# Seven half-size block products for each pair of up-projection chunks, with the weight sums made by accumulating DMAs and the residual rows kept in DRAM

## The chip, the cores and the metric

The kernel runs on one core of a Trainium2 chip. The metric is the device time of one execution in microseconds (us), the median of several runs. All arithmetic is float32; a product that needs float32 accuracy is made of three matmuls of a faster 32-bit type.

## The reference

One layer of a hybrid diffusion model is computed for 640 tokens (128 of a prompt, 512 of a latent grid of width 64). Three mixers on one input projection are merged by gates and projected, a first normalisation follows, and then a gated convolutional feed-forward with a second one. The change lies in the last part:

```python
def _conv_ffn(h, w_up, w_dw, b_dw, w_down, latent):
    a, g = jnp.split(h @ w_up, 2, axis=-1)
    ...   # conv: 3x3 depthwise over the grid (or width 3 on the prompt), of a
    conv = conv + b_dw
    return (jax.nn.gelu(conv) * g) @ w_down

# in _layer
x = _layer_norm(alpha * x + g1 * mix, p['ln1_g'], p['ln1_b'])
h2 = (_norm32(x) * (1.0 + sc2) + sh2)
f = _conv_ffn(h2, p['w_up'], p['w_dw'], p['b_dw'], p['w_down'], latent)
x = _layer_norm(alpha * x + g2 * f, p['ln2_g'], p['ln2_b'])
```

D_MODEL is 1024 and D_FF 2816, so w_up is 1024 x 5632: 22 chunks of 128 columns for a and 22 for g. Chunk j of a and chunk j of g are called pair j here.

## The kernel before

**Split products.** A float32 matrix is held as a high part (a rounded cast, hi) and a low part (the rest, lo). `split` (L219) makes both for a loaded weight chunk of 128 x 1024: ACT casts it into `wh`, and `low` (L195) subtracts on DVE into `wl`. The load is a 512 KB DMA from `wst`, issued on SP into `raw`. `mm3` (L277 to 279) then issues three matmuls: hi by hi, hi by lo, lo by hi. A chunk of the up-projection takes 8 blocks of the inner dimension by 2 halves of 320 tokens by 3, which is 48 matmuls; a pair takes 96.

**The start of the feed-forward.** While the first normalisation is finished, a manual order (all three of PE, DVE and ACT, in `tc.manual_schedule`) transposes and modulates its result into `h2` (eight blocks of 128 x 640, hi and lo; `channel`, `last_channels`), channel by channel. Beside this, the chunks of pairs 0 to 2 are multiplied early: `open_up` loads and splits them, `first_up` issues their matmuls for 384 tokens and later for the other 256, and `land` copies the results from PSUM. `ada_rows` (L443) makes the rows of `g2` from column sums: ACT casts, DVE subtracts, PE sums over partitions by two matmuls with `ones`, and ACT copies from PSUM (L452). The residual `acc` (five tiles of 128 x 1024) lies in SBUF for the whole feed-forward.

**The parts.** The 22 pairs stand in PARTS of 6, 8 and 8. For each part, `expand(j)` calls `raise_` (two chunks by `proj_cm`, each copied from PSUM by ACT in L1511), `taps` (the convolution as one tensor_scalar, L1522, and eleven scalar_tensor_tensor, L1524 and L1534, on DVE) and `weigh` (gelu on ACT, L1540; the product with g on DVE, L1541; cast and low part of the result `h`, L1543 and L195). After the pairs of a part, `contract` multiplies by w_down for ten groups (five token tiles, two halves of 512 columns): 18 or 24 matmuls of 512 columns into PSUM, then two DVE operations (L1557, L1559) that scale by `g2` and add to `acc`. In the last part the second normalisation and the stores follow each token tile.

**The order around it.** Each engine runs its own instructions in order; waits on semaphores join them. Outside the manual blocks a scheduler has interleaved pairs: while PE multiplies pair j, DVE convolves pair j - 1 and splits weights for pair j + 1. `raw` has two buffers, and every third load goes to a third, `raw2`; `wh` and `wl` have four each.

An earlier stage of the kernel already makes products by seven half-size products (its tiles are `pair` and `kept`); its operations on 128 x 320 tiles (L1051, L1055) and its sums of activations (L230) are in the trace.

## Time and profile before

| | |
|---|---|
| time before, median of 3 runs | 1201.14 us (1199.91 to 1201.42) |
| the profiled execution, its own time | 1200.44 us |
| span of the profiled execution | 1198.4 us |
| PE busy | 1179.3 us, 98% of the span |
| DVE busy | 839.8 us, 70% |
| ACT busy | 448.4 us, 37% |
| POOL busy | 0.2 us, no DMA |
| mean granted clock of PE | 0.996 of full speed |
| up-projection matmuls (`up`) | 3 lines, 672 each |

A duration in the trace is that of one instruction from start to end. Instructions of one engine overlap a little, so a row of them takes less than the sum of durations. Where a timeline says `[0.79 <-ACT h L1543]`, the engine stood for 0.79 us until the cast of line 1543 had come. "Hole" in the prediction is a stretch in which PE stands.

### The profile page before, as it was taken

What the parts mean: (1) busy time and instruction counts of PE and PEld (TensorE: products, weight loads), DVE (VectorE), ACT (ScalarE), POOL (GpSimd) and SP (SyncE); (2) the same over time, 40 slices, a digit from 0 to 9 for tenths busy, and PEclk for the clock granted to TensorE, in tenths of its full rate; (3) what the DMA queues carried; (4) which work ended last, traced back from release to release, by engine and by line L of the source; (5) the groups of instructions that cost most, each with busy time, mean ns of one, the idle gap of its engine ahead of it and who ended that gap; (6) DMA issues with size and microseconds to landing.
All of it is one profiled execution on the core that took longest, in us unless ns stands there. A gap on an engine that the chain in (4) does not pass through costs nothing.

```text
span 1198.4 us, 18882 instructions
## 1 busy us (share of the span) xinstructions
PE 1179.3 (98%) x7751; PEld 1120.4 (93%) x7751; DVE 839.8 (70%) x1566; ACT 448.4 (37%) x724; POOL 0.2 (0%) x4
## 2 busy tenths in 40 slices
PE   8999999999999999999999999999999999999996
PEld 7899999999999999989999888898999988999986
DVE  7698666647677658579874678787377764667876
ACT  5566637424344322223333356442133321333320
POOL 0000000000000000000000000000000000000000
PEclk9999999999999999999999999999999999999999
DMA  9431212122125226245442423222222212322221
GB/s 350 181 106 54 71 54 71 54 71 66 49 95 196 90 75 207 89 158 177 145 137 71 158 71 120 75 71 77 82 72 78 81 36 71 124 71 71 72 71 53
DMA packets 35958, 120.35 MB, mean 100 GB/s; under 512 B 4120, under 2 KB 6552, under 8 KB 35872
## 3 DMA queue, kind: packets, MB, share of 16 engines
q1 hardware_dynamic: 35872, 119.16, 29.4%
q8 instruction: 60, 0.98, 0.3%
q14 instruction: 26, 0.21, 0.1%
HBM read 115.47 MB, written 3.67 MB: 99 GB/s over the span
## 4 chain that ended last, share of the span: by engine, by line
PE 88%; DVE 6%; ACT 3%; DMA 2%; issue 1%; SPq 0%; DVEq 0%; ACTq 0%
PE up L278 8%; PE up L277 8%; PE up L279 8%; PE gm L277 5%; PE gm L278 5%; PE gm L279 5%; PE dn L278 4%; PE dn L277 4%; PE dn L279 4%; PE pp L277 2%; PE pp L278 2%; PE pp L279 2%; PE pair L279 1%; PE pair L278 1%; PE rp L279 1%; PE rp L278 1%
## 5 line engine op out<-in xcount | busy, mean ns | idle before, releaser
L219 ACT CAST wh<-raw 128x1024 fp32r<-128x1024 f32 (+1 forms) x137 | 141.8, 1036 | 398.5 <-PE up L278 91.8
L195 DVE TENSOR_TENSOR wl<-raw,wh 128x1024 fp32r<-128x1024 f32 (+1 forms) x141 | 170.2, 1208 | 135.4 <-ACT wh L219 133.9
L278 PE MATMUL up<-go,wh 128*128 128x320 f32 (+2 forms) x672 | 208.7, 311 | 1.1 <-DVE go L195 1.1
L279 PE MATMUL up<-go,wl 128*128 128x320 f32 (+2 forms) x672 | 208.4, 310 | 0.5 <-DVE s11hv L307 0.5
L277 PE MATMUL up<-go,wh 128*128 128x320 f32 (+2 forms) x672 | 208.7, 311 | 0.0
L278 PEld LDWEIGHTS up<-go,wh 128*128 128x128 f32 x672 | 127.0, 189 | 2.2 <-DVE go L195 1.9
L279 PEld LDWEIGHTS up<-go,wl 128*128 128x128 f32 x672 | 126.9, 189 | 0.8 <-DVE wl L195 0.8
L277 PEld LDWEIGHTS up<-go,wh 128*128 128x128 f32 x672 | 127.0, 189 | 0.2
L277 PE MATMUL gm<-h,wh 128*128 128x320 f32 x384 | 121.4, 316 | 0.0
L278 PE MATMUL gm<-h,wh 128*128 128x320 f32 x384 | 119.0, 310 | 0.0
L279 PE MATMUL gm<-h,wl 128*128 128x320 f32 x384 | 118.7, 309 | 0.0
L1534 DVE SCALAR_TENSOR_TENSOR m<-m,par,m 128x441 f32<-128x441 f32 (+2 forms) x152 | 105.6, 695 | 4.1
L421 DVE SCALAR_TENSOR_TENSOR adac<-rawa,csil,adac 128x512 f32<-128x512 f32 x120 | 84.9, 746 | 10.0 <-DMA rawa<-in_wada 7.8
L277 PEld LDWEIGHTS gm<-h,wh 128*128 128x128 f32 x384 | 72.1, 188 | 1.7 <-issue 1.2
L278 PEld LDWEIGHTS gm<-h,wh 128*128 128x128 f32 x384 | 72.2, 188 | 0.3
L279 PEld LDWEIGHTS gm<-h,wl 128*128 128x128 f32 x384 | 72.1, 188 | 0.0
L278 PE MATMUL dn<-wl,h 128*128 128x512 f32 (+1 forms) x188 | 71.4, 381 | 0.0
L279 PE MATMUL dn<-wh,h 128*128 128x512 f32 (+1 forms) x188 | 70.8, 380 | 0.0
L277 PE MATMUL dn<-wh,h 128*128 128x512 f32 (+1 forms) x188 | 70.4, 380 | 0.0
L1557 DVE TENSOR_TENSOR ftmp<-dn,g 128x512 f32<-128x512 f32 (+1 forms) x32 | 20.8, 656 | 45.2 <-PE dn L279 45.2
L278 PEld LDWEIGHTS dn<-wl,h 128*128 128x128 f32 x188 | 35.4, 188 | 7.0 <-DVE wl L195 0.4
L277 PE MATMUL rp<-h,wh 128*128 128x320 f32 x128 | 41.7, 326 | 0.0
(420 smaller groups left out, 2701.3 us busy)
## 6 DMA issues: line engine op xcount, KB each, us to landing
raw<-in_wst SPq DMA_DIRECT2D x152, 512.0 KB, 3.5
rawa<-in_wada SPq DMA_DIRECT2D x32, 512.0 KB, 3.4
wa<-in_wada SPq DMA_DIRECT2D x16, 512.0 KB, 7.6
xa<-in_x SPq DMA_DIRECT2D x5, 512.0 KB, 3.5
xr<-in_x SPq DMA_DIRECT2D x5, 512.0 KB
out_y<-acc SPq DMA_DIRECT2D x10, 256.0 KB, 2.0
ttr<-in_ttab SPq DMA_DIRECT2D x2, 516.0 KB, 6.8
S<-in_state SPq DMA_DIRECT2D x8, 128.0 KB, 3.4
```

What stands on the lines that cost most here:

```text
L195: V.tensor_tensor(out, src, hi.bitcast(F32), op=ALU.subtract)
L219: A.copy(wh[:, 0:n], r)
L277: PE.matmul(out, lhsT=l[0], rhs=r[0], start=start, stop=False, skip_group_check=onto)
L278: PE.matmul(out, lhsT=l[0], rhs=r[1], start=False, stop=False, skip_group_check=onto)
L279: PE.matmul(out, lhsT=l[1], rhs=r[0], start=False, stop=stop, skip_group_check=onto)
L421: MAC.scalar_tensor_tensor(acc_[:, cd], r[:, i], s_, acc_[:, cd], op0=ALU.mult, op1=ALU.add)
L1534: V.scalar_tensor_tensor(cg[:, r0:r1, c0:c1], ag[:, r0 + r - 1:r1 + r - 1, c0 + c - 1:c1 + c - 1], tap(r, c), cg[:, r0:r1, c0:c1], op0=ALU ...
L1557: V.tensor_tensor(ftmp[:, 0:cn], p1[:, 0:cn], g2[:, cd, c], op=ALU.mult)
```

## The change

For pairs 3 to 21 the two chunks of a pair are taken as one product of a 256-column weight matrix with 640 tokens, and the blocks of it (two halves of the inner dimension, a and g, the near 320 and the far 320 tokens) are multiplied in a scheme of seven products of 12 matmuls, in place of eight. The scheme needs sums of weight halves, sums of halves of `h2`, and sums of results.

The weight sums are made by DMAs on POOL: in `up_weights` two 512 KB chunks are loaded on SP into `ra` and `rb`, and five DMAs of 256 KB (four of them accumulating, one a plain load over a used half) turn them into further sets; `r22` is a third load of 256 KB. Four splits give `wa`, `wc`, `wd` (128 x 1024 each) and `wb` (128 x 512). The sums of activations are made once, in `sum_halves` and `low_halves`, in the manual order behind `last_channels`; two more rows of casts and low parts, for the far half of `h2` and for the sums `s4`, stand behind the last `land`. The results are summed in PSUM where the scheme allows it, and otherwise on DVE (L1593, L1600, L1602).

`acc` is stored to DRAM (`x1d`) after the first normalisation, and its SBUF serves the sums and then the buffers `sraw` (5 of 128 x 1024) and `fm` (6 of 128 x 640). `contract` adds to `x1d` by accumulating DMAs on POOL; in the last part the rows are loaded back. `ada_rows` for `g2` becomes `ada_direct`, one float32 matmul in place of cast, low part and two matmuls. The first of the taps moves from DVE to ACT (L1614).

```diff
+FM, SRAW, FT = 6, 5, 2
...
+    def ada_direct(acc_, out, nh):
+        for cd in range(2):
+            pb = p1t("adab")
+            PE.matmul(pb, lhsT=ones.bitcast(F32), rhs=acc_[:, cd], start=True, stop=True)
...
-    accp = ctx.enter_context(tc.tile_pool(name="acc", bufs=1, reuse_waits="tile"))
+    kept_d = ctx.enter_context(tc.tile_pool(name="kd", bufs=1, space=bass.MemoryType.DRAM))
+    x1d = [kept_d.tile([P, D], F32, name=f"x1d{t}") for t in range(NT)]
+    accx = ExitStack()
+    accp = accx.enter_context(tc.tile_pool(name="acc", bufs=1, reuse_waits="tile"))
...
+                    nc.gpsimd.dma_start(out=x1d[t], in_=a)
...
+            s23 = [[mp.tile([P, T], F32R, tag="m", name=nm("s23")) for _ in range(2)] for _ in range(4)]
+            s4_ = [acc[k][:, 640:960] for k in range(4)]
+            s1_ = [acc[4][:, k * 320:(k + 1) * 320] for k in range(3)] + [acc[1][:, 320:640]]
+            def sum_halves(k):
+                x1, x2, s = acc[0][:, 0:T], acc[1][:, 0:T], acc[2 + k % 2][:, 0:T]
+                for x_, a in ((x1, h2[k]), (x2, h2[k + 4])):
+                    V.tensor_tensor(x_, a[0].bitcast(F32), a[1].bitcast(F32), op=ALU.add)
+                s2, s3 = s[:, 0:320], s[:, 320:]
+                V.tensor_tensor(s1_[k], x2[:, 320:], x1[:, 320:], op=ALU.subtract)
+                V.scalar_tensor_tensor(s2, s1_[k], -1.0, x1[:, 0:320], op0=ALU.mult, op1=ALU.subtract)
+                V.tensor_tensor(s3, x1[:, 0:320], x1[:, 320:], op=ALU.subtract)
+                V.scalar_tensor_tensor(s4_[k], s2, -1.0, x2[:, 0:320], op0=ALU.mult, op1=ALU.subtract)
+                A.copy(s23[k][0], s)
+            def low_halves(k):
+                low(s23[k][1], acc[2 + k % 2][:, 0:T], s23[k][0])
+            for k in range(4):
+                sum_halves(k)
+                if k:
+                    low_halves(k - 1)
+            low_halves(3)
...
-            ada_rows(late, g2_sums[0], g2, 0)
+            ada_direct(g2_sums[0], g2, 0)
...
+                hi, lo = sl(h2[k], slice(320, T))
+                A.copy(hi, s1_[k])
+                low(lo, s1_[k], hi)
+            t4 = [late.tile([P, 1024], F32R, tag="adak", bufs=2, name=nm("s4")) for _ in range(2)]
+            u4 = [late.tile([P, 512], F32R, tag=e, bufs=1, name=nm("s4")) for e in ("adah", "adal")]
+            s4 = []
+            for k in range(4):
+                hi, lo = [t[:, k * 320:(k + 1) * 320] for t in t4] if k < 3 else [t[:, 0:320] for t in u4]
+                A.copy(hi, s4_[k])
+                low(lo, s4_[k], hi)
+                s4.append((hi, lo))
+    accx.close()
...
+        def fm():
+            return pu.tile([P, T], F32, tag="fm", bufs=FM, name=nm("fm"))
+        def onto(o, i):
+            nc.gpsimd.dma_start(out=o, in_=i, accum_op=ALU.add)
+        def up_weights(j):
+            ia, ib = (plan.setdefault(("cm", "w_up", i * DFF + j * P), len(plan)) for i in range(2))
+            ra, rb = (pu.tile([P, 1024], F32, tag="sraw", bufs=SRAW, name=nm("sraw")) for _ in range(2))
+            f, s = slice(0, 512), slice(512, 1024)
+            nc.sync.dma_start(out=ra, in_=wst[ia])
+            nc.sync.dma_start(out=rb, in_=wst[ib])
+            wa = split(ra)
+            onto(rb[:, f], wst[ia][:, f])
+            nc.gpsimd.dma_start(out=ra[:, f], in_=wst[ib][:, f])
+            onto(rb[:, s], rb[:, f])
+            onto(ra[:, f], wst[ib][:, s])
+            wc = split(rb)
+            onto(ra[:, s], rb[:, s])
+            r22 = strm.tile([P, 1024], F32, tag="raw", name=nm("raw"))
+            nc.sync.dma_start(out=r22[:, f], in_=wst[ib][:, s])
+            wd = split(ra)
+            wb = split(r22[:, f], 512)
+            return wa, wb, wc, wd
+        near, far = slice(0, 320), slice(320, T)
+        a11, a12 = [[sl(h2[k + i], near) for k in range(4)] for i in (0, 4)]
+        s1, a22 = [[sl(h2[k + i], far) for k in range(4)] for i in (0, 4)]
+        s2, s3 = [sl(s, near) for s in s23], [sl(s, far) for s in s23]
...
-                else:
-                    a = mt()
-                    w = chunk("cm", "w_up", i * DFF + j * P)
-                    pp = ppt("up")
-                    proj_cm(pp, w, h2)
-                    A.copy(tv(a), pv(pp))
-                at.append(a)
-            return at
+                    at.append(a)
+            if at:
+                return at
+            wa, wb, wc, wd = up_weights(j)
+            a, g = fm(), fm()
+            pp = ppt("up")
+            xx, yy, vv = pp[:, 0, 0:320], pp[:, 1, 0:320], p1t("up")[:, 0:320]
+            def product(o, w, c0, acts, new):
+                for k in range(4):
+                    mm3(o, sl(w, slice(c0 + k * P, c0 + (k + 1) * P)), acts[k], bool(new) and k == 0, k == 3, not new)
+            product(xx, wa, 0, a11, 1)
+            A.copy(a[:, near], xx)
+            product(yy, wa, 512, a12, 1)
+            V.tensor_tensor(a[:, near], a[:, near], yy, op=ALU.add)
+            product(xx, wc, 512, s2, 0)
+            A.copy(g[:, near], xx)
+            product(vv, wc, 0, s1, 1)
+            A.copy(a[:, far], vv)
+            product(xx, wd, 0, s3, 0)
+            A.copy(g[:, far], xx)
+            V.scalar_tensor_tensor(g[:, far], g[:, far], -1.0, a[:, far], op0=ALU.mult, op1=ALU.subtract)
+            product(vv, wb, 0, s4, 0)
+            V.scalar_tensor_tensor(g[:, near], g[:, near], -1.0, vv, op0=ALU.mult, op1=ALU.subtract)
+            product(xx, wd, 512, a22, 0)
+            A.copy(a[:, far], xx)
+            return [a, g]
...
-            V.tensor_scalar(cv, a, tap(1, 1), pcol(PB_BDW, j), op0=ALU.mult, op1=ALU.add)
+            A.activation(cv, a, AF.Identity, bias=pcol(PB_BDW, j), scale=tap(1, 1))
...
+            if not last:
+                V.scalar_tensor_tensor(ftmp[:, 0:cn], p1[:, 0:cn], 1.0 / ALPHA, g2[:, cd, c],
+                                       op0=ALU.mult, op1=ALU.mult)
+                onto(x1d[t][:, c], ftmp[:, 0:cn])
+                return
...
+        acc = [pu.tile([P, D], F32, tag="sraw", bufs=SRAW, name=nm("acc")) for _ in range(NT)]
+        for t in range(NT):
+            nc.sync.dma_start(out=acc[t], in_=x1d[t])
+        ln = [[mt()[:, 0:512] for _ in range(2)] for _ in range(2)]
+        for i in range(2):
+            for nh in range(2):
+                nc.sync.dma_start(out=ln[i][nh],
+                                  in_=rows[2 + i:3 + i, nh * 512:(nh + 1) * 512].partition_broadcast(P))
```

First place: ACT, in the manual order behind the activations of the last channel. `adah` and `adab` belong to the rows of g2, `land` is the copy of a raised product, `s_...` are the sums of activations. Before:

```order
L467 ACTIVATE go_7716<-xT_1295_7996,mod 128x256
L447 CAST adah_8057<-adac_6660 128x512
L219 CAST wh_8265<-raw_8263 128x1024
L219 CAST wh_8322<-raw_8320 128x1024
L452 COPY g_7132<-adab_8061 128x512
L447 CAST adah_8065<-adac_6660 128x512
L452 COPY g_7132<-adab_8069 128x512
L1387 COPY land_8073<-up_7564 128x256
L1387 COPY land_8073<-up_7564 128x384
L1387 COPY land_8076<-up_7705 128x256
```

Now:

```order
L474 ACTIVATE go_7726<-xT_1295_8008,mod 128x256
L1498 CAST s_1298_8021<-acc_7129 128x640
L1498 CAST s_1300_8023<-acc_7130 128x640
L1498 CAST s_1302_8025<-acc_7129 128x640
L1498 CAST s_1304_8027<-acc_7130 128x640
L459 COPY g_7139<-adab_8109 128x512
L459 COPY g_7139<-adab_8112 128x512
L1398 COPY land_8115<-up_7574 128x256
L1398 COPY land_8115<-up_7574 128x384
L1398 COPY land_8118<-up_7715 128x256
```

Two weight casts, of chunks of pair 3, and the casts for g2 have gone, and the four casts of the sums stand ahead of the first copies of `adab` and `land`.

Second place: DVE, from the last channel's low parts to the weights of pair 3. Before, where `land` rows are taps of pairs 0 to 2:

```order
L195 TENSOR_TENSOR go_7717<-htmp_8005,go_7716 128x256
L195 TENSOR_TENSOR adal_8058<-adac_6660,adah_8057 128x512
L195 TENSOR_TENSOR wl_8266<-raw_8263,wh_8265 128x1024
L195 TENSOR_TENSOR wl_8323<-raw_8320,wh_8322 128x1024
L195 TENSOR_TENSOR adal_8066<-adac_6660,adah_8065 128x512
L1522 TENSOR_SCALAR m_8208<-land_8073,par 128x640
L1524 SCALAR_TENSOR_TENSOR m_8208<-land_8073,par,m_8208 128x127
L1534 SCALAR_TENSOR_TENSOR m_8208<-land_8073,par,m_8208 128x7x63
L195 TENSOR_TENSOR adal_8130<-adac_6872,adah_8129 128x512
L1524 SCALAR_TENSOR_TENSOR m_8208<-land_8073,par,m_8208 128x127
L1534 SCALAR_TENSOR_TENSOR m_8208<-land_8073,par,m_8208 128x448
L195 TENSOR_TENSOR wl_8398<-raw_8395,wh_8397 128x1024
```

Now, the end of the sums and, further on, the last taps ahead of the first low part of a weight of pair 3 (`sraw`):

```order
L196 TENSOR_TENSOR s_1317_8240<-acc_7127,s_1316_8239 128x320
L196 TENSOR_TENSOR s_1317_8240<-acc_7128,s_1316_8239 128x320
L196 TENSOR_TENSOR s_1317_8240<-acc_7129,s_1316_8239 128x320
L196 TENSOR_TENSOR s_1319_8242<-acc_7130,s_1318_8241 128x320
L1616 SCALAR_TENSOR_TENSOR fm_8257<-land_8115,par,fm_8257 128x127
L1626 SCALAR_TENSOR_TENSOR fm_8257<-land_8115,par,fm_8257 128x7x63
```

```order
L1616 SCALAR_TENSOR_TENSOR fm_8293<-land_7932,par,fm_8293 128x127
L1626 SCALAR_TENSOR_TENSOR fm_8275<-land_7775,par,fm_8275 128x448
L196 TENSOR_TENSOR h_8272<-fm_8257,h_8271 128x640
L1626 SCALAR_TENSOR_TENSOR fm_8275<-land_7775,par,fm_8275 128x7x63
L1626 SCALAR_TENSOR_TENSOR fm_8293<-land_7932,par,fm_8293 128x7x63
L196 TENSOR_TENSOR wl_8316<-sraw_8311,wh_8315 128x1024
```

Taps used to begin while the raised products ran, and weight low parts of pair 3 stood among them; now all taps stand behind the last sum, and 25 rows of pairs 0 to 2 (from L1616 on `fm_8257` to L1626 on `fm_8293`) lie between that sum's low part and the first weight low part of pair 3.

Third place: ACT in the up stage, one pair of part 1 (`sraw_9698` and `sraw_9699` are ra and rb of the next pair, `raw` its r22). Before:

```order
L219 CAST wh_9316<-raw_9314 128x1024
L1511 COPY m_9049<-up_9056 128x640
L1540 ACTIVATE m_9031<-m_9031 128x640
L1543 CAST h_9045<-m_9031 128x640
L219 CAST wh_9373<-raw_9371 128x1024
L1511 COPY m_9106<-up_9113 128x640
L219 CAST wh_9448<-raw_9446 128x1024
L1511 COPY m_9181<-up_9188 128x640
```

Now:

```order
L1614 ACTIVATE fm_9539<-fm_9443,par 128x640
L1591 COPY fm_9584<-up_9586 128x320
L1597 COPY fm_9584<-up_9587 128x320
L220 CAST wh_9702<-sraw_9698 128x1024
L220 CAST wh_9710<-sraw_9699 128x1024
L1595 COPY fm_9585<-up_9586 128x320
L1599 COPY fm_9585<-up_9586 128x320
L1632 ACTIVATE fm_9539<-fm_9539 128x640
L220 CAST wh_9717<-sraw_9698 128x1024
L1635 CAST h_9553<-fm_9539 128x640
L1604 COPY fm_9584<-up_9586 128x320
L220 CAST wh_9721<-raw_9715 128x512
```

And POOL's queue at the same place (before, POOL has no DMA):

```order
L1543 DMA sraw_9699<-in_wst 128x512
L1543 DMA sraw_9699<-sraw_9699 128x512
L1553 DMA sraw_9557<-in_wst 128x512
L1543 DMA sraw_9557<-sraw_9558 128x512
L1543 DMA sraw_9557<-in_wst 128x512
L1543 DMA sraw_9840<-in_wst 128x512
L1543 DMA sraw_9840<-sraw_9840 128x512
L1553 DMA sraw_9698<-in_wst 128x512
```

Of two chunks a pair, ACT now casts three and a half, and copies five halves of results where it copied two wholes; on POOL the two first sums of the pair after next stand ahead of the load and the two sums of the next pair.

## Rows read from the trace of the kernel before

**Rows 1.** The page, parts 1 and 4: busy time, and the chain.

```profile
span 1198.4 us, 18882 instructions
PE 1179.3 (98%) x7751; PEld 1120.4 (93%) x7751; DVE 839.8 (70%) x1566; ACT 448.4 (37%) x724; POOL 0.2 (0%) x4
...
PE 88%; DVE 6%; ACT 3%; DMA 2%; issue 1%; SPq 0%; DVEq 0%; ACTq 0%
```

**Rows 2.** Windows: us, busy (instructions) of PE, PEld, DVE, ACT, POOL; PEclk, DMA share, GB/s.

```profile
750.00:760.00 10.00, 7.92 (x45) 7.07 (x46) 5.20 (x8) 5.51 (x10) 0.00 (x0) 0.83 0.33 105
...
860.00:974.00 114.00, 114.00 (x762) 112.73 (x761) 82.31 (x119) 37.03 (x48) 0.00 (x0) 1.00 0.22 72
974.00:1028.00 54.00, 54.00 (x255) 45.56 (x254) 24.02 (x29) 8.67 (x9) 0.00 (x0) 1.00 0.25 84
1028.00:1142.00 114.00, 114.00 (x760) 112.61 (x759) 83.52 (x122) 38.64 (x51) 0.00 (x0) 1.00 0.22 73
```

**Rows 3.** Timeline of ACT in part 1: start, duration, instruction, [idle before, releaser].

```profile
882.26 1.05 ACT L219 CAST wh<-raw 128x1024 fp32r<-128x1024 f32 x1 [3.06 <-PE up L278]
...
889.30 1.05 ACT L219 CAST wh<-raw 128x1024 fp32r<-128x1024 f32 x1 [5.40 <-issue]
...
896.34 1.05 ACT L219 CAST wh<-raw 128x1024 fp32r<-128x1024 f32 x1 [3.01 <-PE up L278]
```

**Rows 4.** DVE by line and form, 740 us to the end: busy us, mean ns.

```profile
L195 DVE TENSOR_TENSOR wl<-raw,wh 128x1024 fp32r<-128x1024 f32 x56 | 68.5, 1223 | 62.0 <-ACT wh L219 61.2
...
L195 DVE TENSOR_TENSOR h<-m,h 128x640 fp32r<-128x640 f32 x22 | 18.1, 825 | 14.3 <-ACT h L1543 14.3
...
L1524 DVE SCALAR_TENSOR_TENSOR m<-m,par,m 128x127 f32<-128x127 f32 x38 | 13.2, 347 | 0.2
L1522 DVE TENSOR_SCALAR m<-m,par 128x640 f32<-128x640 f32 x19 | 11.5, 608 | 0.0
...
L195 DVE TENSOR_TENSOR go<-raw,go 128x512 fp32r<-128x512 f32 x8 | 5.2, 686 | 0.0
```

**Rows 5.** ACT by line and form, 740 us to the end.

```profile
L219 ACT CAST wh<-raw 128x1024 fp32r<-128x1024 f32 x56 | 58.9, 1051 | 232.0 <-PE up L278 91.8 <-issue 70.2 <-PE dn L279 65.7
...
L1540 ACT ACTIVATE m<-m 128x640 f32<-128x640 f32 x22 | 16.3, 741 | 11.6 <-DVE m L1534 11.6
L1543 ACT CAST h<-m 128x640 fp32r<-128x640 f32 x22 | 16.0, 728 | 25.7 <-DVE m L1541 25.7
...
L1193 ACT CAST go<-raw 128x512 fp32r<-128x512 f32 x8 | 4.5, 618 | 0.5 <-DMA raw<-in_wst 0.5
```

**Rows 6.** Lines and forms, the whole span: operations on 320 and sums of 640.

```profile
L1051 ACT ACTIVATE kept<-pair 128x320 f32<-128x320 f32 x16 | 7.0, 435 | 12.3 <-PE pair L279 12.3
...
L230 DVE TENSOR_TENSOR mixed<-go,go 128x640 f32<-128x640 f32 x8 | 6.2, 822 | 0.1
...
L1055 DVE SCALAR_TENSOR_TENSOR m<-m,kept 128x320 f32<-128x320 f32 x12 | 5.9, 490 | 0.3
```

**Rows 7.** Timeline of DVE, around 750 to 781 us and one pair of part 1.

```profile
749.69 0.43 DVE L195 TENSOR_TENSOR go<-htmp,go 128x256 fp32r<-128x256 f32 x1
...
775.03 6.24 DVE L1534 SCALAR_TENSOR_TENSOR m<-land,par,m 128x504 f32<-128x504 f32 x10
...
893.36 0.83 DVE L195 TENSOR_TENSOR h<-m,h 128x640 fp32r<-128x640 f32 x1 [0.79 <-ACT h L1543]
...
897.42 1.23 DVE L195 TENSOR_TENSOR wl<-raw,wh 128x1024 fp32r<-128x1024 f32 x1 [2.71 <-ACT wh L219]
```

**Rows 8.** Timeline of PE, at the sums for g2.

```profile
755.58 0.50 PE L450 MATMUL adab<-adah,ones 128*128 128x512 f32 x1 [1.55 <-ACT adah L447]
756.43 0.79 PE L451 MATMUL adab<-adal,ones 128*128 128x512 f32 x1 [0.35 <-DVE adal L195]
```

**Rows 9.** Timeline of ACT, at the end of pair 3's first chunk.

```profile
778.04 1.05 ACT L219 CAST wh<-raw 128x1024 fp32r<-128x1024 f32 x1 [4.32 <-PE up L278]
```

**Rows 10.** The page, part 6: DMA issues, KB each, us to landing.

```profile
raw<-in_wst SPq DMA_DIRECT2D x152, 512.0 KB, 3.5
...
out_y<-acc SPq DMA_DIRECT2D x10, 256.0 KB, 2.0
```

40 lines of the change are left out of this document (17 added, 23 removed).

## The prediction

> **What bounds the kernel now.** I read the page first, parts 1 and 4: PE is busy for 1179.3 of 1198.4 us and carries 88% of the chain that ended last, DVE is busy for 70% and ACT for 37% [rows 1]. So only fewer or shorter matmuls, or fewer of PE's waits, can make it faster. The windows then show where this holds most strictly: in the up stage of part 1 PE is busy for all 114 us while DVE is busy for 82.31 and ACT for 37.03; the contraction has DVE at 24.02 of 54 [rows 2]. The timeline of ACT gives the pace: PE releases the weight cast of each chunk at 882.26, 889.30 and 896.34, every 7.04 us [rows 3]. A chunk is 48 matmuls of 320 columns, hence 7.04 / 48 = 0.1467 us each, and a pair of chunks 14.08 us. (The 311 ns that the page's groups show for one matmul is its latency, not its pace.) The sum below is made against the profiled execution, 1200.44 us, of which 1198.4 are span; it lies 0.7 us under the median of 1201.14.
>
> **What it removes.** For pairs 3 to 21 (19 pairs), 2 x 8 x 2 x 3 = 96 matmuls become 7 x 4 x 3 = 84 of the same width. Pairs 0 to 2 are raised early, as before. That is 12 x 0.1467 = 1.76 us of PE a pair, or 33.4 us in all if PE stays the bound at 12.32 us a pair. Nothing else is as large a gain: the direct matmul of ada_direct drops a cast and a low part, whose wait cost PE 1.55 + 0.35 us once [rows 8].
>
> **DVE in the up stage.** Before, a pair costs DVE 82.31 / 114 x 14.08 = 10.17 us. The change adds one low part of 1024 (1.22) and one of 512 (0.69) [rows 4], and three sums of 320 (0.49 each, taken from L1055) [rows 6]; it takes away L1522's tensor_scalar (0.61) [rows 4], which goes to ACT. That makes 10.17 + 1.22 + 0.69 + 1.47 - 0.61 = 12.9 us by durations. Back to back, instructions overlap by a tenth (ten taps in 6.24 us [rows 7], though one takes about 0.7), so 12.4 is the lower end. To that come the waits of DVE that the data force: it stood 0.79 us for the cast of h and, in PE's shadow, 2.71 for the next weight cast [rows 7]. The first stays, so a pair needs about 13.2 us of DVE, more than PE's 12.32. Of 1.76 us, 0.9 is then left.
>
> **The new chain of DMAs.** Nothing on POOL and no accumulating DMA is in the trace. Its price is bounded by hardware transfers: 2.0 us for a 256 KB store, 3.5 for a 512 KB load [rows 10]. A sum reads both operands, as many bytes as the 512 KB load moves, so I take 3.1 us, near the load, and keep 2.0 and 4.5 (the load and one low part more) as ends. Twice a pair this stands in a loop that nothing hides: the low part of the first weights must be done before the third set is loaded over them (L1553), that landing must come before the addition into the same bytes (L1543), and only then can ACT cast the third set. Behind that cast in ACT's queue (third place) stand the cast of h, a copy of 320, the cast of 512, the first tap, two copies of 320 and the next pair's first cast, after which DVE makes its low part. By [rows 5, 6]: 1.05 + 0.73 + 0.44 + 0.62 + 0.74 + 0.44 + 0.44 + 1.05 + 1.22 = 6.7 us, and about 1.5 of the new pair's first product (12 x 0.1467 = 1.76, some of it beside ACT) that the first of those two copies waits for. The loop is 8.2 us plus two transfers: 8.2 + 6.2 = **14.4 us a pair**, against 14.08 now. With 2.0 it is 12.2, and DVE's 13.2 rules; with 3.5 it is 15.2; with 4.5, 17.2. At the start of a part the weights of about two pairs lie ready from the contraction before, so two pairs run at PE's pace (2 x 1.76 = 3.5 us saved) and six by the loop: part 1 and part 2 each gain 3.5 - 6 x 0.32 = 1.5 us. Part 0 has three such pairs, and I give it 3.5.
>
> The Trainium skill, "DMA: Bandwidth & Descriptors", section "Anatomy of one DMA — SWDGE (gpsimd) path", gives a fit of 2.0 us plus bytes over 436e3 for a DMA that GpSimd issues. An estimate by that page is 2.6 us for 256 KB, and the sum would be 13.4 us a pair and about 1209 us; no row here shows such a DMA, and the page's fit is of plain transfers.
>
> **The hole ahead of pair 3.** This is the largest term. sum_halves and its low parts stand in the manual order right behind the last channel's low part, which ends on DVE at 750.0 [rows 7]. Each of four rounds is two additions of 640 (0.82), four operations of 320 (0.49) and a low part of 640 (0.83) [rows 4, 6]: 4.43 us, 17.7 in all by durations, some 16.6 with the overlap, so to 766.6. ACT's queue has the four s23 casts ahead of the copies of adab and of land (first place shown of the order), and the last cast cannot end before about 766.4. PE does the first raised products meanwhile and then waits for those copies to free PSUM. The rest of its raised products, 48 matmuls of 256 columns (0.1467 x 256 / 320 = 0.117 each, 5.7 us), end near 775.6. Only then come the last copies of land, and behind them in ACT's queue eight casts of 320 with a low part each on DVE: 0.4 + 8 x 0.45 + 0.5 is some 4.5 to 5.2 us, hence 780.5. On DVE now follow 25 rows of taps, product and low part of pairs 0 to 2 (second place) before the first weight low part of pair 3: 6 x 0.30 + 17 x 0.62 + 0.82 + 0.83 = 14.0 us. So that low part starts near 794.5 and ends at 795.7, and PE, which has had four matmuls that need no low part, goes on at 796. The loads into sraw do not come before it: their memory is that of acc, which is free at 780.5, and 3.5 us later they have landed. Before, the first chunk of pair 3 ended with the release at 778.04 [rows 9], so it began at 778.04 - 7.04 = 771.0. The hole is **25 us**; part of the old cover was that DVE started these taps at once, in between the raised products. Add 1.6 for the third weights of pair 3, which have to pass POOL twice with nothing else to do, and 1 for matmuls at a lower clock: after waits of 1.9 us the granted clock of 750 to 760 was 0.83 [rows 2, 8]. In all **28 us**.
>
> **What costs nothing.** In the contraction DVE loses one instruction of 0.69 a group, and each accumulation into DRAM has the time of two groups before its buffer is wanted, over 7 us, against at most 4.5; DVE has 30 us idle there [rows 2]. The residual is stored once by POOL and read back during the last up stage, long before it is used. ACT gains about 2 us of copies and 2 us of casts a pair on 37.03 / 114 x 14.08 = 4.6: it is no bound, but its queue's order makes the loop above. The sum: 1200.44 + 28 - 3.5 - 1.5 - 1.5 = **1222 us**.
>
> **Rivals.** *The loop is shorter, DVE is the bound* (13.2 us a pair; transfers of 2.0 to 2.5): parts 1 and 2 gain 3.5 + 6 x 0.88 = 8.8 each, 1200.44 + 28 - 3.5 - 17.6 = 1207. *Transfers are slow* (3.5 and up: POOL's queue is one row, in which the additions of the pair after next stand ahead of this pair's, third place, and an addition can be held by a load): 15.2 a pair costs 3.3 a part, 1231; 17.2 costs 15, 1255. Against it: DMA engines are 22% busy [rows 2]. By the Trainium skill, "SBUF — State Buffer", section "Who interferes with whom", DVE operations with two SBUF inputs hold only GpSimd's reads, and copies and tensor_scalar in their fast modes hold it wholly; by that page the sums and low parts here would not feed this rival, and no trace here shows POOL beside DVE. *PE keeps its pace* (the other side): if DVE's operations overlap enough that a pair takes DVE under 12.4 with its waits, and transfers are near 2.0, all 19 pairs gain 1.76. With 28 of hole this is 1200.44 + 28 - 33.4 = 1195. It decides from a mean period of 12.6 us a pair, 28 / 19 = 1.47 under the old one, and it wants a DVE that hardly ever stands; in the trace it does for over a quarter of that stage [rows 2]. The same rival with half the hole, should the scheduler's taps find gaps, is 1181. *Break-even* between the two, 1198 to 1203, wants the hole near 20 and DVE's pace. That the change does not do what it says can be left out: 84 matmuls a pair stand in PE's order.
>
> **How the numbers follow.** Forecast (1211 to 1231) 0.42; slow transfers 0.21; DVE bound (1203 to 1211) 0.12; break-even 0.07; faster 0.18. The time is the forecast's 1222. The range runs from 1190, within the faster rival, to 1255, and leaves out about 0.09 below and 0.07 above. A measurement of this kernel tells 0.2%, or 2.4 us, from no change: slower 0.42 + 0.21 + 0.12 = 0.75, same 0.07, faster 0.18.
>
> **What would show it.** Right: PE idle for some 20 us or more between 755 and 800, with DVE's first weight low part of pair 3 after 790; pair periods of 13 to 15 us in parts 1 and 2, PE waiting there for the third weights' casts and low parts; contractions of 54 us as before; POOL's additions at 2.5 to 3.5 us. Wrong: pair 3 started before 785, periods of 12.3, additions above 4.5 us, or a contraction that has grown because its buffer waits for a landing.

## The result, and the profile after

The changed kernel takes 1316.91 us, median of 4 runs (1315.29 to 1317.9), against 1201.12 before: a ratio of 1.0965, 95% interval 1.0946 to 1.0984. It is slower, as forecast, but by 116 us and not by 21. The page of the changed kernel, its parts 1, 4 and 6, beside [rows 1, 10]:

```profile
span 1313.5 us, 19102 instructions
...
PE 1193.1 (91%) x7523; PEld 1117.9 (85%) x7523; DVE 886.2 (67%) x1651; ACT 510.4 (39%) x849; POOL 97.0 (7%) x124
...
PE 64%; DMA 13%; DVE 9%; issue 6%; ACT 5%; POOL 1%; SPq 0%; DVEq 0%; ACTq 0%; POOLq 0%
...
sraw<-in_wst SPq DMA_DIRECT2D x38, 512.0 KB, 4.8
...
sraw<-in_wst POOLq DMA_DIRECT2D x57, 256.0 KB, 4.5
sraw<-sraw POOLq DMA_DIRECT2D x38, 256.0 KB, 3.7
...
x1d<-ftmp POOLq DMA_DIRECT2D x20, 256.0 KB, 3.9
```

PE's matmuls have become fewer (7523 for 7751), yet PE is busy for 91% of a span that is 115.1 us longer, and only 64% of the chain is PE's; 13% is DMA, which was 2%. The DMAs of POOL land 3.7 to 4.5 us after their issue, and the hardware's loads into `sraw` need 4.8 us.

Where the time came from is read by stages. The scalings of a contraction (`ftmp`) mark them; the first ones of parts 0 and 1 in the timeline of DVE, before:

```profile
825.20 1.29 DVE L1557 TENSOR_TENSOR ftmp<-dn,g 128x512 f32<-128x512 f32 x2 [3.38 <-PE dn L279]
...
978.43 1.29 DVE L1557 TENSOR_TENSOR ftmp<-dn,g 128x512 f32<-128x512 f32 x2 [3.33 <-PE dn L279]
```

and after:

```profile
872.52 1.29 DVE L1650 SCALAR_TENSOR_TENSOR ftmp<-dn,g 128x512 f32<-128x512 f32 x2 [0.63 <-PE dn L280]
...
1057.65 1.29 DVE L1650 SCALAR_TENSOR_TENSOR ftmp<-dn,g 128x512 f32<-128x512 f32 x2 [0.76 <-PE dn L280]
```

The last ones start at 855.08 and 1022.40 before, at 901.79 and 1098.82 after. Up to the first contraction 872.52 - 825.20 = 47.3 us are lost. Inside the first contraction the difference is -0.6 (29.27 for 29.88 us), in the up stage of part 1 +32.5 (155.86 for 123.35), in the second contraction -2.8 (41.17 for 43.97), and the rest, up stage of part 2 and the end, is 115.1 - 76.4 = 38.7. So nothing is lost in the contractions; of the 115, 71 are in the up stages of parts 1 and 2 (the end with them) and 47 in and before that of part 0.

The windows show what PE does there (columns as in [rows 2]):

```profile
760.00:770.00 10.00, 5.20 (x25) 3.42 (x23) 7.57 (x14) 4.32 (x9) 0.00 (x0) 0.79 0.00 0
...
780.00:790.00 10.00, 0.90 (x2) 0.50 (x2) 9.97 (x21) 4.31 (x6) 0.90 (x1) 0.50 0.72 262
...
990.00:1050.00 60.00, 49.34 (x272) 46.16 (x272) 42.84 (x65) 26.52 (x41) 9.83 (x12) 0.89 0.63 158
1150.00:1200.00 50.00, 39.79 (x234) 38.09 (x233) 35.23 (x54) 21.62 (x35) 11.61 (x15) 0.89 0.62 142
```

Between 760 and 800 PE is busy for 14.4 us in all, and from 780 to 800 its granted clock is 0.50. In parts 1 and 2, where the stage had PE busy for all 114 us [rows 2], it is busy for 80 to 82%, DVE for 70 to 71%, ACT for 43 to 44%, and the DMA engines for 62 to 63% where they had 22%. No engine is the bound there; PE waits.

Why it waits is read from the chain of one pair in part 1. In the chain that ended last (start, duration, what) stand:

```profile
972.00 4.24 DMA sraw<-in_wst
...
983.56 4.45 DMA sraw<-in_wst
```

and in the timeline of POOL, the same pair, with the loads over the first weights (L1553) of three pairs in a row:

```profile
967.64 0.58 POOL L1553 DMA_DIRECT2D sraw<-in_wst  x1 [1.38 <-DVE wl L196]
968.21 0.91 POOL L1543 DMA_DIRECT2D sraw<-sraw  x1
...
976.80 0.87 POOL L1543 DMA_DIRECT2D sraw<-in_wst  x1 [5.04 <-DMA sraw<-in_wst]
982.63 0.85 POOL L1543 DMA_DIRECT2D sraw<-sraw  x1 [4.96 <-DMA sraw<-in_wst]
983.56 0.58 POOL L1553 DMA_DIRECT2D sraw<-in_wst  x1
984.13 0.90 POOL L1543 DMA_DIRECT2D sraw<-sraw  x1
988.30 0.85 POOL L1543 DMA_DIRECT2D sraw<-in_wst  x1 [3.27 <-DMA sraw<-in_wst]
...
1002.51 0.58 POOL L1553 DMA_DIRECT2D sraw<-in_wst  x1 [1.37 <-DVE wl L196]
```

At 968.21 POOL issues a pair's sum into the second half of `ra`, the last reader of that pair's `rb`. Its landing lets SP load the `rb` of the pair after next (issue 972.00, landed 976.2). On it POOL makes the first sum at 976.80, waits 4.96 us for it to land, and only then, since its queue is in order, can it issue the load for the next pair's third weights (983.56), whose landing the sum into the same bytes waits for (988.30). From 968.21 to the same sum of the next pair at 984.13 pass 15.9 us, of which 13.8 are three landings in a row: 3.8, 4.2 and 5.8. The split of the third weights starts at 992.5; from there the chain goes on through ACT's queue to L1591 at 995.89 and to the next product.

So there are two rings. One is that of the queue and the buffers, as just followed. The other is the pair's own loop, the one that the prediction summed: from the load over the first weights through its landing, the sum into the same bytes, the cast of the third weights, ACT's queue, and the next pair's first cast and low part to the next such load. The rows of L1553 tell which of the two is the longer. At 967.64 and at 1002.51 POOL had been free for 1.4 us when DVE's low part released the load. Of the six rounds of part 1 that begin with the load at 912.46, five end with such a wait, of 0.3 to 3.2 us, and in the sixth (983.56) both rings come out together. In the middle of the part the pair's own loop thus sets the pace, and the queue's ring is close behind it. At the start of the part the queue holds: the low part was done at 907.4, and the load stood until 912.46 behind a first sum of a later pair.

### The profile page after: what moved, and what is told of

The parts are those of the page before. It is cut to its first block, busy times and chain, and to the rows that moved or that the text cites. A ratio compares the mean times of both kernels' runs of the same rounds, so it can differ in the third digit from the quotient of the medians.

```text
span 1313.5 us, 19102 instructions
## 1 busy us (share of the span) xinstructions
PE 1193.1 (91%) x7523; PEld 1117.9 (85%) x7523; DVE 886.2 (67%) x1651; ACT 510.4 (39%) x849; POOL 97.0 (7%) x124
## 4 chain that ended last, share of the span: by engine, by line
PE 64%; DMA 13%; DVE 9%; issue 6%; ACT 5%; POOL 1%; SPq 0%; DVEq 0%; ACTq 0%; POOLq 0%
DMA sraw<-in_wst 10%; PE gm L278 4%; PE gm L279 4%; PE gm L280 4%; PE dn L279 3%; PE dn L278 3%; PE dn L280 3%; PE up L278 2%; DVE wl L196 2%; PE up L279 2%; PE up L280 2%; PE pp L278 2%; PE pp L279 2%; PE pp L280 2%; DMA raw<-in_wst 2%
## 5 line engine op out<-in xcount | busy, mean ns | idle before, releaser
L278 PE MATMUL up<-go,wh 128*128 128x320 f32 (+2 forms) x368 | 127.4, 349 | 88.9 <-ACT fm L1591 60.0
L220 ACT CAST wh<-raw 128x1024 fp32r<-128x1024 f32 (+1 forms) x118 | 113.4, 964 | 209.8 <-PE gm L279 91.4
L196 DVE TENSOR_TENSOR wl<-raw,wh 128x1024 fp32r<-128x1024 f32 (+1 forms) x122 | 136.6, 1121 | 80.2 <-ACT wh L220 79.3
L278 PEld LDWEIGHTS up<-go,wh 128*128 128x128 f32 x368 | 76.9, 209 | 98.1 <-ACT fm L1591 64.9
L220 ACT CAST wh<-sraw 128x1024 fp32r<-128x1024 f32 x57 | 59.7, 1047 | 189.7 <-DMA sraw<-in_wst 77.3
L196 DVE TENSOR_TENSOR wl<-sraw,wh 128x1024 fp32r<-128x1024 f32 x57 | 69.6, 1223 | 84.8 <-ACT wh L220 84.6
L280 PE MATMUL up<-go,wl 128*128 128x320 f32 (+2 forms) x368 | 122.1, 335 | 3.3 <-DVE wl L196 2.9
L279 PE MATMUL up<-go,wh 128*128 128x320 f32 (+2 forms) x368 | 123.5, 336 | 1.1 <-DVE go L196 1.1
L1626 DVE SCALAR_TENSOR_TENSOR fm<-fm,par,fm 128x441 f32<-128x441 f32 (+2 forms) x152 | 105.2, 692 | 1.8
L280 PEld LDWEIGHTS up<-go,wl 128*128 128x128 f32 x368 | 77.3, 211 | 4.1 <-DVE wl L196 3.3
L279 PEld LDWEIGHTS up<-go,wh 128*128 128x128 f32 x368 | 77.7, 211 | 2.3 <-DVE go L196 2.0
L278 PE MATMUL up<-s,wh 128*128 128x320 f32 x228 | 76.0, 337 | 0.1
L278 PE MATMUL dn<-wh,h 128*128 128x512 f32 (+1 forms) x188 | 71.7, 386 | 3.3 <-ACT wh L220 3.3
L279 PE MATMUL up<-s,wh 128*128 128x320 f32 x228 | 74.1, 326 | 0.0
```

Of the source, the lines that this page charges most:

```text
L196: V.tensor_tensor(out, src, hi.bitcast(F32), op=ALU.subtract)
L220: A.copy(wh[:, 0:n], r)
L278: PE.matmul(out, lhsT=l[0], rhs=r[0], start=start, stop=False, skip_group_check=onto)
L279: PE.matmul(out, lhsT=l[0], rhs=r[1], start=False, stop=False, skip_group_check=onto)
L280: PE.matmul(out, lhsT=l[1], rhs=r[0], start=False, stop=stop, skip_group_check=onto)
L1626: V.scalar_tensor_tensor(cg[:, r0:r1, c0:c1], ag[:, r0 + r - 1:r1 + r - 1, c0 + c - 1:c1 + c - 1], tap(r, c), cg[:, r0:r1, c0:c1], op0=ALU ...
```

## The experiments

"A pair" below is the mean of the last six of seven distances between the copies L1591 (or its line in the kernel) in part 1; the changed kernel has 17.7 us there.

**The weight sums left out.** Only the five DMAs of POOL go:

```diff
-            onto(rb[:, f], wst[ia][:, f])
-            nc.gpsimd.dma_start(out=ra[:, f], in_=wst[ib][:, f])
-            onto(rb[:, s], rb[:, f])
-            onto(ra[:, f], wst[ib][:, s])
...
-            onto(ra[:, s], rb[:, s])
```

> All five POOL DMAs of each pair are left out; the three loads, the four splits, the seven products and all of DVE's and ACT's work stay (the weights are not summed, so the products are of other numbers). Theory 1, the up stage waits for the chain of POOL's DMAs (17.4 us a pair in the trace of the changed kernel): a pair falls to what DVE needs, 12.9 to 13.5 us, in parts 1 and 2, PE stays idle around 760 to 800 us as now, and the span falls by 75 to 105 us, to 1208 to 1238 us. Rival, DVE's added work or the order in ACT's queue is the bound and the DMAs only fill its gaps: a pair stays above 16 us and the span above 1290.

1216.62 us, a span of 1214.9. The copies of the first product, in the timeline of ACT, and the windows of that stage:

```profile
920.44 0.41 ACT L1586 COPY fm<-up 128x320 f32<-128x320 f32 x1
...
933.86 0.41 ACT L1586 COPY fm<-up 128x320 f32<-128x320 f32 x1
...
900.00:960.00 60.00, 59.18 (x385) 56.14 (x385) 56.50 (x85) 34.88 (x55) 0.00 (x0) 1.00 0.33 98
```

A pair takes 13.35 us, PE is busy for 59.2 of 60 us and DVE for 56.5: both are nearly full, though PE starts a matmul only every 0.16 us (60 / 385) and not every 0.147. Theory 1 holds: the weights' DMAs on POOL cost 98.6 of the 115 us, in one run. (The scheduler orders every one of these kernels anew, so an edit can move instructions in other queues too; where that matters below, it is said.)

**The sums of activations left out.** sum_halves, low_halves and the later casts go, and the products take blocks of h2:

```diff
-            for k in range(4):
-                sum_halves(k)
...
-        s2, s3 = [sl(s, near) for s in s23], [sl(s, far) for s in s23]
+        s2, s3 = a11, a22
+        s4 = a12
```

> sum_halves, low_halves and the eight casts with low parts behind the last land copy are left out; the products take blocks of h2 in the place of the sums. Weight sums stay. Theory 1: PE's hole between 760 and 800 us goes, pair 3 begins at 770 to 778 us, and the span falls by 22 to 30 us, to 1283 to 1292; pairs of parts 1 and 2 keep 17 to 18 us. Rival, the hole is covered by the wait for the weights of pair 3 through POOL: the span falls by under 10 us, to 1303 or more.

1285.67 us, a span of 1283.9: 29.6 less. **Both left out:**

> Both left out. Theory 1 adds up: 1313 - 90 - 26, a span of 1180 to 1212 us; the up stages of parts 1 and 2 take 12.4 to 13.5 us a pair. If PE's saved 1.76 us a pair are kept whole (12.3 us a pair), it is 1165 to 1180. Rival, each sum's wait hides the other's: the two falls do not add, and the span stays above 1225.

1195.18 us, a span of 1193.4, 21.5 under the kernel without weight sums alone. PE in the 50 us from 750, in the kernel without either, without weight sums, and in the changed one:

```profile
750.00:800.00 50.00, 46.30 (x301) 42.38 (x301) 40.65 (x65) 26.20 (x44) 0.00 (x0) 0.97 0.30 96
...
750.00:800.00 50.00, 27.23 (x152) 22.94 (x152) 39.59 (x70) 19.99 (x36) 0.00 (x0) 0.74 0.16 58
...
750.00:800.00 50.00, 23.90 (x140) 19.44 (x140) 34.61 (x66) 17.69 (x33) 3.51 (x4) 0.73 0.24 70
```

46.3, 27.2 and 23.9 us of 50 (before, 47.9 in a window of the same bounds). The hole is the activation sums'. Alone the two costs are 98.6 and 29.6, together 1313.5 - 1193.4 = 120.1: 8 us of the two overlap. What is left when both are free is 1195.18 against 1201.96 in the same call, one run each: less than 7 us of the 33 that PE no longer has to work.

**POOL's DMAs copying in place of adding.**

```diff
-            nc.gpsimd.dma_start(out=o, in_=i, accum_op=ALU.add)
+            nc.gpsimd.dma_start(out=o, in_=i)
```

> POOL's DMAs stay, with their waits and order, but copy in place of adding (so the weights are not the sums and the residual is not added). Theory 1a, the price is that of a DMA through POOL's queue and of its landing: landing times stay within 0.5 us of now (4.5 for a load, 3.7 within SBUF), a pair stays at 16 us or more, the span above 1295. Rival, the addition itself (the second read) is the price: landings of 3.5 us or less, a pair at 14.5 to 15.5, a span of 1250 to 1285.

**Their order that of the code** (POOL's queue under a manual order, so that the first sums of a later pair stand behind this pair's; ACT's order changed with it, as shown below):

```diff
-    with tc.tile_pool(name="pu", bufs=1, reuse_waits="tile") as pu:
+    with tc.tile_pool(name="pu", bufs=1, reuse_waits="tile") as pu, tc.manual_schedule(engines={mybir.EngineType.Pool}):
```

> POOL's DMAs stand in the order of the code (per pair: first sum, load, second sum, and so on; those of the next pair behind them); nothing else is changed. Theory 2, what sets 17.4 us a pair is the queue: the first sum of the pair after next, which waits for a load into bytes that the last sum of an earlier pair frees, holds the load and the sums of the next pair. Then that ring is gone, a pair falls to 14 to 16.5 us (the chain of load, sum and split remains), the span to 1270 to 1300. Rival, the landings alone set it, in any order: a pair stays at 17 us or more, the span at 1305 or more.

**And both at once**, to ask for the size of the loop:

> POOL's DMAs in the order of the code, as in pool_in_program_order, and copying in place of adding (the weights are not the sums). It asks for the size of the loop. Theory 2a, in that order only the chain of one pair is left (low part of the first weights, load, last sum, split of the third weights, casts, next low part): 7.7 us beside the DMAs, 9.7 us in them in pool_in_program_order; copies land in 3.5 us in place of 3.3 to 4.8, so 7.7 + 7.0 to 7.6 = 14.7 to 15.3 us a pair, a span of 1262 to 1285. Rival, something else has a period of 16.4 us and more (as in both of the single changes): 16.4 or more again, a span above 1290.

Landing times, from part 6 of the page of the copying kernel (the one in the code's order has 4.2, 4.2 and 4.1):

```profile
sraw<-in_wst POOLq DMA_DIRECT2D x57, 256.0 KB, 3.5
sraw<-sraw POOLq DMA_DIRECT2D x38, 256.0 KB, 3.5
...
x1d<-ftmp POOLq DMA_DIRECT2D x20, 256.0 KB, 2.4
```

| | adding | copying |
|---|---|---|
| POOL's order as scheduled | 17.7 us a pair, 1316.91 us | 16.5 us a pair, 1284.29 us |
| the order of the code | 16.7 us a pair, 1309.12 us | 14.8 us a pair, 1265.27 us |

For the copies I expected landings that stay, and the rival had it right: 3.5 us, at the place of 4.5, 3.7 and 3.9. The 57 DMAs of the first line are 38 sums and 19 plain loads (L1553); the sums alone land after 4.6 us in the median, and after 3.4 as copies. So the addition costs 1.2 us from DRAM to SBUF, 0.2 within SBUF and 1.5 into DRAM. The kernel fell to 1284, at the rival's edge, but the pair only to 16.5. For the order, the 16.7 us a pair lie between the two theories' ranges, and the time is the rival's, since the first pairs of a part now stand behind all DMAs of the contraction (the first distance in part 1 is 29.5 us, and 22.5 in the changed kernel). The two changes take 1.2 and 1.0 us off a pair, together 2.9, and 14.8 lies in the range of theory 2a.

What each of them shortens is read from the pair's own loop, in part 1, as means of five or six rounds in us:

| | adding, as scheduled | copying, as scheduled | adding, order of the code | copying, order of the code |
|---|---|---|---|---|
| the load (L1553) to the third weights' cast (L220) | 8.5 | 7.5 | 9.7 | 8.2 |
| this cast to the copy L1591 | 3.0 | 3.1 | 1.5 | 1.5 |
| L1591 to the next load | 6.3 | 5.7 | 5.8 | 5.3 |
| one round | 17.8 | 16.3 | 16.9 | 14.9 |

Two loads of POOL, the cast and L1591 of one round, with copies as scheduled; then this cast and L1591 with copies in the order of the code:

```profile
950.95 0.55 POOL L1553 DMA_DIRECT2D sraw<-in_wst  x1 [3.74 <-DVE wl L196]
966.77 0.55 POOL L1553 DMA_DIRECT2D sraw<-in_wst  x1 [2.90 <-DVE wl L196]
...
958.22 1.05 ACT L220 CAST wh<-sraw 128x1024 fp32r<-128x1024 f32 x1 [1.60 <-DMA sraw<-in_wst]
961.46 0.41 ACT L1591 COPY fm<-up 128x320 f32<-128x320 f32 x1
```

```profile
968.23 1.04 ACT L220 CAST wh<-sraw 128x1024 fp32r<-128x1024 f32 x1 [1.28 <-DMA sraw<-sraw]
969.18 0.61 ACT L220 CAST wh<-raw 128x512 fp32r<-128x512 f32 x1
969.70 0.42 ACT L1591 COPY fm<-up 128x320 f32<-128x320 f32 x1
```

In the three variants every such load of these rounds waits for the low part: 2.2 to 3.7 us with copies as scheduled, 9.1 to 11.1 us in the order of the code. So the queue's ring sets the pair in none of them, and the 16.5 us with copies are the pair's own loop. Nor is the gain of the other order shown to be the queue's: that order also took the cast of h, the copy L1604 and the first tap out from between the third weights' cast and L1591 in ACT's queue. This stretch fell by 1.5 and 1.6 us, more than the round did (0.9 and 1.4); the stretch ahead of it grew.

**The sums as four additions of 128x512**, on DVE and then on POOL, with the finished `rc` in the place of r22:

```diff
+            rc = strm.tile([P, 1024], F32, tag="raw", name=nm("raw"))
+            V.tensor_tensor(rc[:, f], ra[:, f], rb[:, f], op=ALU.add)
+            V.tensor_tensor(rc[:, s], rc[:, f], rb[:, s], op=ALU.add)
+            V.tensor_tensor(ra[:, f], rb[:, f], rb[:, s], op=ALU.add)
             wc = split(rc)
+            V.tensor_tensor(ra[:, s], ra[:, s], rc[:, s], op=ALU.add)
             wd = split(ra)
             wb = split(rb[:, s], 512)
```

> The weight sums are four additions of 128x512 on DVE (0.69 us each, 0.62 back to back), r22 and all weight DMAs of POOL go; the results are as before. Theory 1, DVE is what bounds the up stage when the DMA chain is away (13.42 us a pair without sums): a pair takes 13.4 + 4 x 0.62 to 0.69 = 15.9 to 16.2 us, the span is 1250 to 1270. Rival, DVE has slack that takes them in: 13.4 to 14.5 us, a span under 1235.

> The same four additions as instructions on POOL. No trace of this kernel has such an instruction. If one takes under 1.5 us and leaves DVE alone, a pair stays at 13.4 to 14 us and the span at 1212 to 1228. Rival, POOL and DVE hold each other up: then DVE's instructions in that stage get longer by up to the duration of POOL's, 3 us a pair or more, a pair takes 16 us or more, and the span is above 1250.

On DVE 1233.29 us with 14.3 us a pair, within the rival's numbers: of the 2.5 us that four additions take, only 0.9 are seen in the mean. The last three pairs of part 1 take 15.0 us each, and in two of them DVE hardly stands:

```profile
951.91:981.83 29.92, 26.14 (x168) 24.66 (x168) 29.29 (x48) 15.33 (x26) 0.00 (x0) 1.00 0.27 88
```

That is 0.3 us of standing a pair, so an estimate of DVE's whole need without the additions is 15.0 - 0.3 - 2.5 = 12.2 us, and the 13.35 of the kernel without weight sums hold some 1.2 us of waits. On POOL 1266.11 us with 15.9 us a pair, as the rival had it. The forms by line of POOL there, and of DVE in the same stage:

```profile
L1557 POOL TENSOR_TENSOR sraw<-sraw,raw 128x512 f32<-128x512 f32 x19 | 32.2, 1697 | 0.0
...
L1553 POOL TENSOR_TENSOR raw<-sraw,sraw 128x512 f32<-128x512 f32 x18 | 24.8, 1376 | 99.7 <-DMA sraw<-in_wst 63.4 <-DVE fm L1624 26.2 <-ACT fm L1593 6.5
...
L1624 DVE SCALAR_TENSOR_TENSOR fm<-fm,par,fm 128x441 f32<-128x441 f32 x14 | 14.2, 1017 | 0.3
...
L196 DVE TENSOR_TENSOR wl<-raw,wh 128x1024 fp32r<-128x1024 f32 x4 | 7.5, 1881 | 1.9 <-ACT wh L220 1.9
```

One addition of 512 takes POOL 1.4 to 1.7 us, and DVE's taps of 441 take 1017 ns (676 in the kernel without weight sums), its low parts up to 1881 for 1223 [rows 4]: DVE's instructions get longer beside POOL's. What POOL's take alone no run shows. The Trainium skill, "SBUF — State Buffer", section "Who interferes with whom", states that a DVE instruction with two SBUF inputs contends with a GpSimd instruction that reads SBUF; these rows agree.

**The residual's DMAs left out**, to see whether they keep the first pairs of a part from lying ready:

```diff
-                onto(x1d[t][:, c], ftmp[:, 0:cn])
```

> The twenty accumulating DMAs of the contractions are left out (the residual lacks parts 0 and 1). Theory 3, they hold the weight sums of the next part's first pairs in POOL's queue, so that no pair lies ready at a part's start: the span falls by 8 to 25 us, to 1288 to 1305, all of it between the contractions and the first two pairs of parts 1 and 2. Rival, they are hidden: within 4 us of 1313.

1309.85 us: 5.4 us of span in one run, between the two forecasts and nearer the rival's. The first distance in part 1 fell from 22.5 to 19.2 us, and a pair kept 18.0. They share the queue, but most of what keeps the first pairs waiting is there without them.

**The sums made early, in DRAM.** POOL makes `wc` and `wd` of all pairs from DRAM to DRAM, and the up stage loads them:

```diff
+            for src in (wst[ia], c_, d_):
+                r = pu.tile([P, 1024], F32, tag="sraw", bufs=SRAW, name=nm("sraw"))
+                nc.sync.dma_start(out=r, in_=src)
+                out.append(split(r))
```

> The same weight sums are made by POOL's DMAs from DRAM to DRAM between 320 and 730 us, before anything needs them, and the up stage loads three and a half finished chunks a pair on SP. Theory 1: pairs at 13.4 us as without sums, PE's hole before pair 3 stays, span 1212 to 1226. Rival, the 133 early DMAs slow the loads and waits of the stages beside them, or the three loads from the new place arrive late: above 1235.

1244.78 us. A pair takes 13.3 us, as expected, but the rival holds too: the gate that should have kept the DMAs back opened too early, POOL issued them within the first 320 us, and there PE was busy for 296 us where it had been for 315. **The scheme from part 1 on**, with such sums, part 0 as before, and the sums of activations in part 0's contraction:

> Sums in DRAM as in sums_ahead_in_dram; part 0 is raised as before the change (two chunks a pair), and the sums of activations are made during part 0's contraction, where DVE stood for over half the time before. Theory 1: the hole goes, pairs of parts 1 and 2 take 12.9 to 13.4 us in place of 14.08, so 16 x 0.7 to 0.9 = 11 to 14 us are saved, against some 2 to 4 us for the first pair of part 1, whose buffers the sums use until late: 1187 to 1196 us, faster than both. Rival, the sums hold the contraction's own DVE operations and the first weights of part 1: 1198 us or more.

1223.99 us, 1.0193 (1.0172 to 1.0214) times the kernel before: the forecast of 1187 to 1196 fell. **The same with three places mended:**

> As scheme_from_part_1, with three places mended that its trace showed: the DMAs that make the sums in DRAM start behind the stage of w_gla_out (some 330 us) and go one pair at a time, so that they do not fill the DMA engines at 120 to 250 us; the first chunk of the second half of w_down is split ahead of the sums; part 0 uses its old buffers. Theory 1: what was lost there (13 us before 320 us, 10 us of PE's wait for a weight in the contraction, some 5 us in part 0) comes back, pairs of parts 1 and 2 take 13.4 us: 1190 to 1200 us. Rival, the sums of activations hold the contraction whatever the order, or the DMAs cost the stages beside them the same later: 1204 us or more.

1222.43 us (1219.23 to 1233.6), 1.0175 (1.0149 to 1.0201) times the kernel before: the forecast of 1190 to 1200 fell. The windows of this kernel, in the execution of 1233.6 us, the longest of the six:

```profile
320.00:400.00 80.00, 74.55 (x501) 73.99 (x500) 50.79 (x77) 30.48 (x46) 16.97 (x25) 0.96 0.76 201
400.00:500.00 100.00, 94.09 (x645) 91.22 (x644) 60.59 (x101) 25.58 (x42) 24.45 (x35) 0.95 0.83 203
500.00:600.00 100.00, 86.43 (x492) 79.85 (x492) 61.76 (x126) 20.92 (x25) 22.05 (x31) 0.91 0.86 231
600.00:700.00 100.00, 94.01 (x626) 92.95 (x625) 62.62 (x84) 28.86 (x39) 15.47 (x22) 0.97 0.65 171
860.00:900.00 40.00, 39.81 (x180) 32.41 (x178) 30.79 (x52) 11.30 (x18) 7.69 (x9) 1.00 0.63 140
```

The scheme itself does what it should: a pair takes 13.3 us, the contraction with the sums in it has PE busy for 39.8 of 40 us, and from the first matmul of part 1's up stage (897.3, before 854.0) to the end pass 334.5 us, 9.9 less than the 344.4 before. But the DMAs that make the sums keep the DMA engines at 0.65 to 0.86 from 320 to 700 us, and there PE is busy for 349 of 380 us, at a clock of 0.91 to 0.97; before it was busy for 379. Loads of the kernel itself get slower beside them (`rawa` lands after 6.7 us, in the kernel before after 3.4). In this execution part 1 begins 43 us later than before, 30 of which PE stands between 320 and 700, and 10 us are won behind. No version here that makes the sums beats the kernel before. Sums made on DVE in stages where it stands, and stored, were not tried.

## Why the prediction was wrong in size

**The hole: right.** The last low part of the sums was forecast for 766.6 and ended at 767.7, the casts behind the last land copy for 780.5, and DVE's last of these low parts ended at 781.5. The timeline of DVE:

```profile
766.16 1.55 DVE L196 TENSOR_TENSOR s<-acc,s 128x640 fp32r<-128x640 f32 x2
...
779.84 1.69 DVE L196 TENSOR_TENSOR s<-acc,s 128x320 fp32r<-128x320 f32 x4
...
797.62 0.82 DVE L196 TENSOR_TENSOR h<-fm,h 128x640 fp32r<-128x640 f32 x1 [4.50 <-ACT h L1635]
...
799.54 1.22 DVE L196 TENSOR_TENSOR wl<-sraw,wh 128x1024 fp32r<-128x1024 f32 x1
```

The first weight low part of pair 3 was forecast for 794.5 and came at 799.5, held by the cast of h, which stood in ACT's queue behind the second set's cast, which waited 5.1 us for a sum to land. Instead of 25 us the delay of pair 3 is 800.8 - 771.0 = 29.8 us; I had 28 with its surcharges. Taken away in experiments it is 21.5 to 29.6.

**DVE as the bound without the DMAs: right in size, not in reason.** 13.2 us a pair were forecast and 13.35 measured. But DVE's need is some 12.2, and the rest is waits. (My lower end of 12.4 does not follow from its rows: a tenth off the 3.4 us that come in leaves 12.6.) The reason that a pair does not reach PE's 12.32 I take to be the order in which copies, low parts and products wait for each other, with DVE at 94%; this is read from the rows and not tested. The number was in part luck.

**The pair's loop: the step that failed, in its sizes.** The loop that I summed is the one that sets a pair in the middle of a part, but its 14.4 us (two landings of 3.1 and 8.2 beside them) are 17.8 in the trace: 8.5 for 6.2 from the load to the third weights' cast, and 9.3 for 8.2 from there to the next load. In part 1 the load lands after 3.0 to 4.8 us and the sum after 4.0 to 4.9, where I took 3.1 from [rows 10]; for a copy that is near (3.5 into SBUF). The addition adds 1.2 us. The rest I put down to DMA engines that are 60% busy: loads on SP into the same buffers land in 4.8 us, in 3.6 without the weights' DMAs. My upper end of 4.5, 17.2 a pair, was near the 17.7, and my own sign of being wrong, additions above 4.5 us, came true at 4.6.

An estimate by the Trainium skill, "DMA: Bandwidth & Descriptors", section "Anatomy of one DMA — SWDGE (gpsimd) path", is 2.6 us for 256 KB. Here only the copies into DRAM, at 2.4, are that fast; for copies into SBUF the measured 3.5 stands in its place.

**The queue's ring: named and not priced.** I named POOL's single queue among the rivals but priced only the landings in it. The queue joins two pairs: the first sum of the pair after next waits for a load that waits for the last sum of an earlier pair, and behind it stands the next pair's load. That ring is 15.9 us in the pair shown, with no work of PE, DVE or ACT in it. It does not set the pair in the middle of a part, where the pair's own loop is as long or longer; at the start of a part it does.

**The two pairs that lie ready: wrong.** I gave each part 3.5 us for them, and so forecast for 17.2 us a pair 15 us a part. The first distances in parts 1 and 2 are 22.5 and 23.1 us, the longest of their stages, where I had 12.3. Without the weight sums they are 12.9, so it is the sums that are not ready. In part 1 the load stands for 5 us in the queue there (from 907.4 to 912.46). With five buffers a pair's `rb` also waits for the sums of the second pair ahead of it; more buffers were not tried, so this is read from the order and not shown. Without the residual's DMAs ahead in the queue the distance is 19.2. Seven distances of 128.7 us in part 1 against 7 x 14.08 are 30.1 of the 32.5 us that the stage lost. Of what I missed there, six distances of 17.7 for 14.4 make 20 us and the first one 10.

**The clock.** I counted 1 us once. In six of the seven pairs of part 1 that follow its first, the first 13 to 20 matmuls behind PE's wait run at the lower of its two levels, 1.2 GHz, 0.267 us apart and not 0.147. Two pairs in the timeline of PE, and the windows behind these matmuls:

```profile
961.39 0.64 PE L278 MATMUL up<-go,wh 128*128 128x320 f32 x1 [4.07 <-ACT fm L1591]
...
978.71 0.41 PE L278 MATMUL up<-go,wh 128*128 128x320 f32 x1 [1.88 <-ACT fm L1591]
```

```profile
961.80:967.00 5.20, 5.20 (x21) 5.20 (x21) 3.85 (x7) 1.04 (x1) 0.85 (x1) 0.50 0.66 190
...
979.10:984.40 5.30, 5.30 (x39) 5.30 (x38) 5.23 (x9) 1.89 (x2) 1.69 (x3) 1.00 0.69 196
```

At 961.39 PE had stood for 4.07 us, and its granted clock is 0.50 behind that; at 978.71 it had stood for 1.88, and the clock stays at 1.00. The loop's stretch from L1591 to the next load takes 5.3 us in the round at full clock and 6.0 to 6.7 in the others, so the clock makes 0.7 to 1.4 us of a pair's 17.7.

**What cost nothing: right, nearly.** The contractions are 0.6 and 2.8 us shorter, and the residual's DMAs cost 5.4 us of 115.

The forecast's own sum with the measured sizes is: 29.8 for the hole, 17.5 from pair 3 to the first contraction (71.7 us for 54.2, with distances of 15.7 and 27.9 us between the pairs), 32.5 and 38.7 for the two parts, less 3.4 in the contractions: 115.1. The forecast had its sign from the hole alone. Either of the two costs makes the kernel slower by itself (1216.62 us with the hole alone, 1285.67 with the weight sums alone), so the right sign says little for the sum; three quarters of the size came from terms that stood in it as gains.
